# Strided attention: merged preparation, declared waits, and V loaded from the GpSimd queue

## The chip, the cores and the metric

The kernel runs on one core of a Trainium2 chip. A core has five instruction streams: TensorE (PE in the profile; its weight loads are PEld), VectorE (DVE), ScalarE (ACT), GpSimd (POOL) and SyncE (SP), and 16 DMA engines that carry data between the chip's memory and the core's SBUF. The metric is the device time in microseconds (us); lower is better. The times of the kernel before are 128.76, 128.98 and 129.75 us, with a median of 128.98.

## The reference: what is computed

Q, K and V have the shape 8 x 12 x 1024 x 64 in float32, and the stride is 64. Every query attends only to the 16 positions 0, 64, 128, ..., 960:

```
for i in range(seq):
    attend_positions = np.arange(0, seq, stride)
    q = Q[:, :, i:i + 1, :]
    k = K[:, :, attend_positions, :]
    v = V[:, :, attend_positions, :]
    scores = einsum('bhqd,bhkd->bhqk', q, k) * scale          # scale = 1/8
    weights = exp(scores - max(scores)); weights /= sum(weights) + 1e-10
    result[:, :, i, :] = einsum('bhqk,bhkd->bhqd', weights, v)
```

All of Q (25.2 MB) is read and all of the result (25.2 MB) is written. Of K and V only one row in 64 is read, 0.39 MB each, in rows of 64 floats (256 bytes) that lie 16 KB apart.

## The kernel before, in words

The 96 pairs of batch and head are worked on in 24 groups (`g`) of four heads. A group loads 1 MB of Q into one of ten buffers `qn` (`load`, L95), and stores 1 MB of the result from one of eight buffers `out_sb` (`store`, L243). Both are DMAs that SyncE issues, all on one queue and in the order in which the program names them: K, Q0, V, Q1 to Q9, and then in the loop store 0, Q10, store 1, Q11 and so on, and at the end only stores. Each of these DMAs also waits until the one eight places before it has landed.

The order of work on each engine is written out by hand (`manual_schedule`); the framework adds the waits between engines from what is read and written. Per group:

- `cast` (L188): Q is turned to bf16 in two halves, one on POOL (L191), one on ACT (L192), into one of two buffers `qb`.
- `transpose` (L194): DVE transposes it in 32 x 32 blocks into `qt` (L196).
- `scores` (L198): four matmuls against the zero-padded keys `k_t` (L203), then two exponentials on ACT (L214) into one of three weight buffers in `w_all`.
- `values` (L180): POOL multiplies a mask with the group's values into one of three buffers in `v_all` (L182). Four more columns of `v_all` give the sums of the weights.
- `outputs` (L221): eight matmuls (L228) in three parts (`c`). DVE takes the reciprocals of the sums (L236) and multiplies the first two parts (L238); for the third part ACT copies it out of PSUM (L240) and POOL multiplies it in place (L241).

The function `ahead` runs the transpose, the values and the scores of later groups before the outputs of the current one, and `cast` three groups ahead.

Ahead of the loop stand the preparations. POOL builds an identity matrix (L120, L121), copies of its columns `perm_v` (L128), and clears two thirds of `k_t` (L134). DVE clears the rest (L132) and `w_all` (L133), and builds the mask from an iota in four small operations (L136 to L139). `key_rows` (L147) casts four of K's twelve slices on ACT and transposes them on DVE; `keys` (L156) places them in `k_t` with four small copies for each half. The first four slices are done ahead of the loop, with half of the copies on DVE; the others in two lots within groups 1 to 3 and 5 to 7. V is cast on DVE (L258), and `value_rows` (L168) spreads six of its slices at a time with two matmuls (L171), each with a copy out of PSUM on DVE (L175): ahead of the loop and again in group 4.

`addr_align(128, max_nops=0)` (L87 for DVE and POOL, L102 for SyncE) makes an engine's stream go on at an aligned place in the instruction memory, by a jump.

Of the kernel before, what the change touches and what calls it, by code (L numbers as in the profile page):

```python
# [9 lines left out]

FP32 = mybir.dt.float32
BF16 = mybir.dt.bfloat16
I16 = mybir.dt.int16
I32 = mybir.dt.int32
AF = mybir.ActivationFunctionType
ALU = mybir.AluOpType
# [8 lines left out]
def _copy(nc, out: bass.AP, in_: bass.AP):  # L25

    sides = [
        mybir.BassSymbolicTensorAccessPattern(
            ap=side.ap, dtype=side.dtype, bass_ap=side,
            is_dma=True, for_custom_bir_dma=True,  # L30
        )
        for side in (in_, out)
    ]
    return nc.sync.add_instruction(
        mybir.InstDMACopy(
            name=nc.get_next_instruction_name(), engine=mybir.EngineType.SP,
            ins=sides[:1], outs=sides[1:], queue="qSPDynamicHW",
            mode="Copy",
        )
    )  # L40
# [9 lines left out]
def kernel(  # L50
# [8 lines left out]
    nc = tc.nc  # L59

    B, H, S, D = Q.shape
    NK = S // stride
# [3 lines left out]
    HG = 4  # L66
# [6 lines left out]
    OBUFS = 8  # L73

    const = ctx.enter_context(tc.tile_pool(name="const", bufs=1))
    qn_pool = ctx.enter_context(tc.tile_pool(name="qn", bufs=QBUFS))
    out_pool = ctx.enter_context(tc.tile_pool(name="outsb", bufs=OBUFS))
    qb_pool = ctx.enter_context(tc.tile_pool(name="qb", bufs=2))
# [12 lines left out]
    v_raw = const.tile([P, NC, D], FP32, name="v_raw")  # L91
    kv_src = [[stride * D, P], [2 * HG * SD, NC], [1, D]]
    qn = {}

    def load(g):  # L95
        qn[g] = qn_pool.tile([P, 32 * D], FP32, name="qn", tag="qn")
        n = P if g < 2 else 32
        _copy(nc, qn[g], _ap_with(Q, [[HG * SD // n, n], [1, HG * SD // n]], g * HG * SD))
# [10 lines left out]
    ahead4 = const.tile([P, 4], I16, name="ahead4")  # L109
    slot4 = const.tile([P, 4], I16, name="slot4")  # L110
# [15 lines left out]
    for c in range(2):  # L126
        for a in range(2):
# [5 lines left out]
    nc.vector.memset(w_all, 0.0)  # L133
    nc.gpsimd.memset(k_t[:, 8:NG], 0.0)  # L134

    nc.vector.tensor_single_scalar(out=slot4, in_=ahead4, scalar=48, op=ALU.bitwise_and)  # L136
# [7 lines left out]
    v_rep = const.tile([P, NC, 2, D], BF16, name="v_rep")  # L144


    def key_rows(m):  # L147
        part = slice(4 * m, 4 * m + 4)
# [7 lines left out]
    def keys(m, c):  # L156
        for s in range(4):
            src, dst, col = 32 * (2 * c + s % 2), 32 * (2 * (s % 2) + s // 2), NK + 32 * s
            op = nc.vector.tensor_copy if m == 0 and s >= 2 else nc.scalar.copy
            op(  # L160
                k_t[dst : dst + 32, 8 * m + c : 8 * m + 8 : 2, :, col : col + NK],
                k_r[src : src + 32, 4 * m : 4 * m + 4].rearrange(
                    "p n (a k f) -> p a n f k", a=2, f=2
                )[:, s // 2],
            )


    def value_rows(n):  # L168
        for c in range(2):
            vp = psum_sc.tile([P, NC // 2, D], FP32, name="vp", tag="sc")  # L170
            nc.tensor.matmul(  # L171
                vp, lhsT=perm_v[:, c].rearrange("p a b e k -> p (a b e k)"),
                rhs=v_bf[:, 6 * n : 6 * n + 6], start=True, stop=True,
            )
            nc.vector.tensor_copy(out=v_rep[:, 6 * n : 6 * n + 6, c], in_=vp)  # L175

    qb, qt, wt, vb, rec, out_sb = {}, {}, {}, {}, {}, {}


    def values(g):  # L180
        vb[g] = v_bufs[g % 3]
        nc.gpsimd.tensor_tensor(  # L182
            out=vb[g][:, 0 : 4 * D].rearrange("p (s d) -> p s d", s=4), in0=mask,
            in1=v_rep[:, g // 2, g % 2].unsqueeze(1).to_broadcast([P, 4, D]),
            op=ALU.mult,
        )

    def cast(g):  # L188
        qb[g] = qb_pool.tile([P, 32 * D], BF16, name="qb", tag="qb")
        half = 16 * D  # L190
        nc.gpsimd.tensor_copy(out=qb[g][:, 0:half], in_=qn[g][:, 0:half])  # L191
        nc.scalar.copy(qb[g][:, half:], qn[g][:, half:])  # L192

    def transpose(g):  # L194
        qt[g] = qt_pool.tile([P, 32 * D], BF16, name="qt", tag="qt")
        nc.vector.transpose(qt[g].bitcast(I32), qb[g].bitcast(I32))  # L196

    def scores(g):  # L198
        sc = psum_sc.tile([P, 512], FP32, name="sc", tag="sc")
        q = qt[g]  # L200
        for e in range(2):
            for f in range(2):
                nc.tensor.matmul(  # L203
                    sc, lhsT=k_t[:, g, f, NK * (1 - e) : NK * (1 - e) + P],
                    rhs=_ap_with(
                        q, [q.ap[0], [D, 8], [16 * D, 2], [2, 32]],
                        extra_offset=8 * D * e + f,
                    ),
                    start=e + f == 0, stop=e + f == 2,
                )  # L210
        w = wt[g] = w_bufs[g % 3]
        for a in range(2):
            wa = w[64 * a : 64 * a + 64]
            nc.scalar.activation(  # L214
                out=_ap_with(wa, [wa.ap[0], [P, 8], [1, 2], [2, 32]], extra_offset=64 * a),
                in_=sc[64 * a : 64 * a + 64].rearrange("p (t x q) -> p t x q", t=8, x=2),
                func=AF.Exp, bias=0.0, scale=scale,
            )


    def outputs(g, c):  # L221
        if c == 0:
            out_sb[g] = out_pool.tile([P, 4, 8, D], FP32, name="out_sb", tag="out_sb")
# [12 lines left out]
        nc.vector.reciprocal(r, ps[:, 0:n, 4 * D : 4 * D + 4])  # L236
        if c < 2:
            nc.vector.tensor_tensor(out=to, in0=o, in1=by, op=ALU.mult)  # L238
        else:
            nc.scalar.copy(to, o)  # L240
            nc.gpsimd.tensor_tensor(out=to, in0=to, in1=by, op=ALU.mult)  # L241

    def store(g):  # L243
        o = out_sb[g]
        _copy(
            nc,
            _ap_with(out, [[16 * D, P], [2 * SD, 2], [1, 16 * D]], g * HG * SD),
            _ap_with(o, [o.ap[0], [1, 1], [1, 32 * D]]),
        )

    key_rows(0)
    keys(0, 0)
    cast(0)
    transpose(0)
    keys(0, 1)
# [19 lines left out]
    for g in range(NG):  # L275
        if g > 0:
            ahead(g)
        for c in range(3):
            outputs(g, c)
        if g == 0:  # L280
            ahead(g)
        if g in (1, 5):
            key_rows(g // 4 + 1)
        if g in (2, 3, 6, 7):
            keys(g // 4 + 1, g % 4 - 2)
        if g == 4:
            value_rows(1)
        store(g)
        if g + QBUFS < NG:
            load(g + QBUFS)  # L290
# [33 lines left out]
```

## Time and profile before

| | |
|---|---|
| median of 3 runs | 128.98 us (128.76 to 129.75) |
| the profiled execution's own time | 128.94 us |
| its span, first to last instruction | 127.2 us |
| mean granted TensorE clock | 0.835 |
| busy: PE, DVE, ACT, POOL | 51%, 69%, 68%, 62% of the span |
| moved by DMA | 51.20 MB, of it 25.95 MB read from memory and 25.17 MB written |
| issue to landing, median: Q load, store, K, V | 14.7, 13.5, 4.5, 7.4 us |

The span is one profiled execution; the 1.74 us between it and that execution's time lie ahead of the first instruction or behind the last. "Busy" counts instructions that do work; DMA issues and waits are not in it. A line of the table by stage gives a stretch in us, its length, the busy time of PE, PEld, DVE, ACT and POOL with the count of instructions, the clock granted to TensorE, the mean busy share of the 16 DMA engines (it can be a little over 1, as packets overlap) and the GB/s that they moved. A line in order of time gives start, duration, engine, line, operation, output and input, and in brackets the idle time before it and what ended it. "SPq" is SyncE issuing DMAs; the transfer itself comes later.

### The profile page before, as it was taken

How to read it: one execution, taken by the hardware profiler on the slowest of the kernel's cores; microseconds unless marked ns; L12 is line 12 of the kernel's file. 1: busy time of each engine (PE TensorE's matmuls, PEld its weight loads, DVE VectorE, ACT ScalarE, POOL GpSimd, SP SyncE). 2: the span in 40 equal slices, each digit the busy share in tenths (PEclk: the TensorE clock that was granted, in tenths of full speed). 3: DMA queues.
4: the chain of work that ended last, by engine and by line, in shares of the span. 5: the costliest groups of instructions: out<-in, count | busy, mean ns of one | idle time of the engine just before them, and what ended most of it. 6: DMA issues, size and time to landing. Idle time of an engine off the chain costs nothing.

```text
span 127.2 us, 1226 instructions
## 1 busy us (share of the span) xinstructions
PE 64.3 (51%) x292; PEld 30.2 (24%) x292; DVE 88.4 (69%) x162; ACT 86.0 (68%) x120; POOL 79.5 (62%) x84
## 2 busy tenths in 40 slices
PE   0006548196757619662787636666463797430000
PEld 0002223042323304330333313233232343110000
DVE  4956592769698786877887889797988876760000
ACT  4151917957999986999958997979798765620000
POOL 6941818645855994595867896969889673454000
PEclk9999999755699995999657999999999558975555
DMA  2999999989998998998999989989999999999980
GB/s 67 374 329 474 464 412 423 464 381 394 451 451 381 459 464 343 487 433 376 500 387 405 497 353 438 461 374 451 428 402 451 397 433 420 425 433 417 428 350 26
DMA packets 7911, 51.20 MB, mean 403 GB/s; under 512 B 3872, under 2 KB 3872, under 8 KB 3872
## 3 DMA queue, kind: packets, MB, share of 16 engines
q1 hardware_dynamic: 7904, 51.12, 96.5%
q8 instruction: 2, 0.03, 0.1%
q14 instruction: 5, 0.04, 0.1%
HBM read 25.95 MB, written 25.17 MB: 402 GB/s over the span
## 4 chain that ended last, share of the span: by engine, by line
POOL 35%; issue 32%; DMA 15%; DVE 4%; PE 2%; ACT 1%; POOLq 1%; SPq 0%; DVEq 0%
POOL qb L191 14%; POOL out_sb L241 12%; POOL v_all L182 9%; DMA out_dram<-out_sb 9%; DMA qn<-in_Q_dram 5%; PE sc L203 1%; POOLq L319 1%; DVE out_sb L238 1%; DVE qt L196 1%; DVE v_rep L175 1%; ACT qb L192 1%; PE vp L171 1%; ACT out_sb L240 1%; DVE rec L236 0%; SPq L100 0%
## 5 line engine op out<-in xcount | busy, mean ns | idle before, releaser
L228 PE MATMUL o_ps<-v_all,w_all 128*128 128x260 bf16 x192 | 38.4, 320 | 37.1 <-DVE out_sb L238 32.8
L241 POOL TENSOR_TENSOR out_sb<-out_sb,rec 128x768 f32<-128x768 f32 x24 | 35.3, 1471 | 29.8 <-ACT out_sb L240 29.8
L238 DVE TENSOR_TENSOR out_sb<-o_ps,rec 128x768 f32<-128x768 f32 (+1 forms) x48 | 39.6, 825 | 1.7
L214 ACT ACTIVATE w_all<-sc 64x512 bf16<-64x512 f32 x48 | 35.2, 734 | 5.5 <-PE sc L203 4.9
L203 PE MATMUL sc<-qt,k_t 128*128 128x512 bf16 x96 | 32.0, 466 | 10.7 <-DVE qt L196 10.7
L196 DVE STREAM_TRANSPOSE qt<-qb 128x1024 int32<-128x1024 int32 x24 | 29.6, 1232 | 10.8 <-ACT qb L192 5.7
L228 PEld LDWEIGHTS <-w_all 128*128 128x128 bf16 x192 | 18.9, 109 | 60.3 <-DVE out_sb L238 41.2
L240 ACT COPY out_sb<-o_ps 128x768 f32<-128x768 f32 x24 | 19.2, 798 | 16.1 <-DVE rec L236 15.8
L191 POOL CAST qb<-qn 128x1024 bf16<-128x1024 f32 x24 | 24.9, 1036 | 4.7 <-DMA qn<-in_Q_dram 4.7
L192 ACT CAST qb<-qn 128x1024 bf16<-128x1024 f32 x24 | 25.0, 1045 | 0.7
L236 DVE RECIPROCAL rec<-o_ps 128x12 f32<-128x12 f32 (+1 forms) x72 | 15.1, 210 | 6.3 <-PE o_ps L228 5.8
L182 POOL TENSOR_TENSOR v_all<-mask,v_rep 128x256 bf16<-128x256 bf16 x24 | 16.0, 668 | 0.6 <-DVE v_rep L175 0.6
L203 PEld LDWEIGHTS <-k_t 128*128 128x128 bf16 x96 | 10.8, 113 | 21.6 <-ACT k_t L160 8.1
L160 ACT COPY k_t<-k_r 32x128 bf16<-32x128 bf16 x20 | 5.9, 295 | 2.1 <-DVE k_r L150 1.9
L134 POOL MEMSET k_t<- 128x4608 bf16 x1 | 3.9, 3938 | 0.0
L175 DVE CAST v_rep<-vp 128x384 bf16<-128x384 f32 x4 | 2.2, 542 | 1.9 <-PE vp L171 1.8
L149 ACT CAST k_bf<-k_raw 128x256 bf16<-128x256 f32 x3 | 1.2, 406 | 3.2 <-DMA k_raw<-in_K_dram 3.2
L150 DVE STREAM_TRANSPOSE k_r<-k_bf 128x128 int32<-128x128 int32 x3 | 0.9, 310 | 2.3 <-ACT k_bf L149 2.3
L136 DVE TENSOR_SCALAR slot<-ahead 128x4 int16<-128x4 int16 x1 | 2.5, 2482 | 0.0
L171 PE MATMUL vp<-v_bf,perm_v 128*128 128x384 bf16 x4 | 1.6, 412 | 1.1 <-DVE v_rep L175 0.6
L132 DVE MEMSET k_t<- 128x1152 uint32 x1 | 1.0, 1018 | 1.6 <-PEq L305 1.6
L149 ACT ACT_TABLE_LOAD x1 | 1.3, 1283 | 0.7 <-PEq L305 0.7
(15 smaller groups left out, 5.7 us busy)
## 6 DMA issues: line engine op xcount, KB each, us to landing
qn<-in_Q_dram SPq DMA_DIRECT2D x24, 1024.0 KB, 14.7
out_dram<-out_sb SPq DMA_DIRECT2D x24, 1024.0 KB, 13.5
k_raw<-in_K_dram SPq DMA_DIRECT2D x1, 384.0 KB, 4.5
v_raw<-in_V_dram SPq DMA_DIRECT2D x1, 384.0 KB, 7.4
```

Source lines behind the costliest of these rows:

```text
L160: op(k_t[dst : dst + 32, 8 * m + c : 8 * m + 8 : 2, :, col : col + NK], k_r[src : src + 32, 4 * m : 4 * m + 4].rearrange("p n (a k f) -> p ...
L182: nc.gpsimd.tensor_tensor(out=vb[g][:, 0 : 4 * D].rearrange("p (s d) -> p s d", s=4), in0=mask, in1=v_rep[:, g // 2, g % 2].unsqueeze(1).t ...
L191: nc.gpsimd.tensor_copy(out=qb[g][:, 0:half], in_=qn[g][:, 0:half])
L192: nc.scalar.copy(qb[g][:, half:], qn[g][:, half:])
L196: nc.vector.transpose(qt[g].bitcast(I32), qb[g].bitcast(I32))
L203: nc.tensor.matmul(sc, lhsT=k_t[:, g, f, NK * (1 - e) : NK * (1 - e) + P], rhs=_ap_with(q, [q.ap[0], [D, 8], [16 * D, 2], [2, 32]], extra_ ...
L214: nc.scalar.activation(out=_ap_with(wa, [wa.ap[0], [P, 8], [1, 2], [2, 32]], extra_offset=64 * a), in_=sc[64 * a : 64 * a + 64].rearrange( ...
L228: nc.tensor.matmul(ps[:, i, 0 : 4 * D + 4], lhsT=wt[g][:, i0 + i], rhs=vb[g], start=True, stop=True,)
L236: nc.vector.reciprocal(r, ps[:, 0:n, 4 * D : 4 * D + 4])
L238: nc.vector.tensor_tensor(out=to, in0=o, in1=by, op=ALU.mult)
L240: nc.scalar.copy(to, o)
L241: nc.gpsimd.tensor_tensor(out=to, in0=to, in1=by, op=ALU.mult)
```

## The change

V's load moves from SyncE's queue to POOL's, and its position there is ahead of POOL's other preparation. The aligning jumps are taken out on all three engines.

The preparation is merged. All of `k_t` is cleared by one memset on DVE. The mask comes from one reduction over the identity on DVE and two copies on POOL, in place of an iota and four operations on DVE. The remaining eight slices of K are cast and transposed in one lot in group 1, and their copies, eight in place of sixteen, go two to a group in groups 2 to 5. The first key copies that were on DVE are on POOL, and V's cast too; on POOL it stands behind the cast of Q1. The two matmuls of `value_rows` write two banks of one PSUM tile of the output pool, and one copy on DVE takes both.

Buffers that came from rotating pools (`qn`, `qb`, `out_sb`) are fixed tiles, and dependencies that follow from others are declared as none (`implied`): a reloaded Q buffer on its old load and casts, a cast on the casts two groups before, exponentials and values on those of three groups before, and ACT's copy and POOL's product on the store that used the buffer last. In exchange the transpose of group `g`, for `g` of 10 and more, waits for store `g - 10`, which frees the buffer that DVE fills next.

```diff
-    for engine in (nc.vector, nc.gpsimd):
-        engine.addr_align(128, max_nops=0)
...
+    def implied(ins, earlier, why):
+        tc.declare_no_dep(ins.ins, earlier.ins, reason=why)
...
     nc.sync.dma_start(k_raw, _ap_with(K, kv_src))
     load(0)
-    nc.sync.addr_align(128, max_nops=0)
-    nc.sync.dma_start(v_raw, _ap_with(V, kv_src))
+    nc.gpsimd.dma_start(v_raw, _ap_with(V, kv_src))
...
-    nc.gpsimd.iota(ahead4, pattern=[[-16, 4]], base=64, channel_multiplier=1)
...
-    nc.vector.memset(k_t[:, 0:8], 0.0)
+    nc.vector.memset(k_t, 0.0)
     nc.vector.memset(w_all, 0.0)
-    nc.gpsimd.memset(k_t[:, 8:NG], 0.0)
-
-    nc.vector.tensor_single_scalar(out=slot4, in_=ahead4, scalar=48, op=ALU.bitwise_and)
-    nc.vector.tensor_single_scalar(out=s_sel, in_=slot4, scalar=0, op=ALU.is_equal)
-    nc.vector.tensor_copy(out=v_all[:, :, 4 * D :], in_=s_sel.unsqueeze(1).to_broadcast([P, 3, 4]))
-    nc.vector.tensor_copy(out=mask, in_=s_sel.unsqueeze(2).to_broadcast([P, 4, D]))
+
+    nc.vector.tensor_reduce(
+        out=s_sel, in_=identity.rearrange("p (h s k) -> p s h k", h=2, s=4),
+        op=ALU.max, axis=mybir.AxisListType.XY,
+    )
+    nc.gpsimd.tensor_copy(out=v_all[:, :, 4 * D :], in_=s_sel.unsqueeze(1).to_broadcast([P, 3, 4]))
+    nc.gpsimd.tensor_copy(out=mask, in_=s_sel.unsqueeze(2).to_broadcast([P, 4, D]))
...
-            op = nc.vector.tensor_copy if m == 0 and s >= 2 else nc.scalar.copy
+        op = nc.gpsimd.tensor_copy if part is first and s >= 2 else nc.scalar.copy
...
     def value_rows(n):
+        vp = psum_o.tile([P, 3, 512], FP32, name="o_ps", tag="o")
+        rows = vp[:, 0:2, 0 : NC // 2 * D].rearrange("p c (n d) -> p c n d", d=D)
         for c in range(2):
-            vp = psum_sc.tile([P, NC // 2, D], FP32, name="vp", tag="sc")
...
-            nc.vector.tensor_copy(out=v_rep[:, 6 * n : 6 * n + 6, c], in_=vp)
+        nc.vector.tensor_copy(
+            out=v_rep[:, 6 * n : 6 * n + 6].rearrange("p n c d -> p c n d"), in_=rows
+        )
...
+        if g - 2 >= OBUFS:
+            tc.add_manual_dep(
+                turned.ins, stored[g - 2 - OBUFS].ins.name,
+                mybir.DependencyInfo(mybir.DependencyClass.Sync, mybir.DependencyReason.ANTI),
+                reason="frees the output buffer that VectorE fills next",
+            )
...
     cast(1)
-    nc.vector.tensor_copy(out=v_bf, in_=v_raw)
+    nc.gpsimd.tensor_copy(out=v_bf, in_=v_raw)
     value_rows(0)
...
-        if g in (1, 5):
-            key_rows(g // 4 + 1)
-        if g in (2, 3, 6, 7):
-            keys(g // 4 + 1, g % 4 - 2)
+        if g == 1:
+            key_rows(rest)
+        if 2 <= g < 6:
+            for i in range(2 * g - 4, 2 * g - 2):
+                keys(rest, i // 4, i % 4)
```

More of the change, by code (lines that the diff above doesn't have):

```diff
@@ L12 @@
 BF16 = mybir.dt.bfloat16
-I16 = mybir.dt.int16
 I32 = mybir.dt.int32
@@ L84 @@
     ctx.enter_context(tc.manual_schedule())
-    for engine in (nc.vector, nc.gpsimd):
-        engine.addr_align(128, max_nops=0)
     k_raw = const.tile([P, NC, D], FP32, name="k_raw")
     v_raw = const.tile([P, NC, D], FP32, name="v_raw")
+    qn_bufs = [const.tile([P, 32 * D], FP32, name=f"qn{i}") for i in range(QBUFS)]
+    qb_bufs = [const.tile([P, 32 * D], BF16, name=f"qb{i}") for i in range(2)]
+    out_bufs = [const.tile([P, 4, 8, D], FP32, name=f"out_sb{i}") for i in range(OBUFS)]
     kv_src = [[stride * D, P], [2 * HG * SD, NC], [1, D]]
-    qn = {}
+    qn, stored, cast_by, scaled = {}, {}, {}, {}
+    loaded, raised, masked = {}, {}, {}
+    def implied(ins, earlier, why):
+        tc.declare_no_dep(ins.ins, earlier.ins, reason=why)
     def load(g):
-        qn[g] = qn_pool.tile([P, 32 * D], FP32, name="qn", tag="qn")
+        qn[g] = qn_bufs[g % QBUFS]
         n = P if g < 2 else 32
-        _copy(nc, qn[g], _ap_with(Q, [[HG * SD // n, n], [1, HG * SD // n]], g * HG * SD))
+        loaded[g] = _copy(nc, qn[g], _ap_with(Q, [[HG * SD // n, n], [1, HG * SD // n]], g * HG * SD))
+        if g >= QBUFS:
+            for earlier in (loaded[g - QBUFS], *cast_by[g - QBUFS]):
+                implied(loaded[g], earlier, "the store before it has waited for both casts")
     nc.sync.dma_start(k_raw, _ap_with(K, kv_src))
     load(0)
-    nc.sync.addr_align(128, max_nops=0)
-    nc.sync.dma_start(v_raw, _ap_with(V, kv_src))
+    nc.gpsimd.dma_start(v_raw, _ap_with(V, kv_src))
     for g in range(1, QBUFS):
@@ L144, with key_rows @@
     v_rep = const.tile([P, NC, 2, D], BF16, name="v_rep")
-    def key_rows(m):
-        part = slice(4 * m, 4 * m + 4)
+    def key_rows(part):
         nc.scalar.copy(k_bf[:, part], k_raw[:, part])
@@ L186, in values @@
         )
+        if g >= 3:
+            implied(masked[g], masked[g - 3], "the matmuls between them")
     def cast(g):
-        qb[g] = qb_pool.tile([P, 32 * D], BF16, name="qb", tag="qb")
+        qb[g] = qb_bufs[g % 2]
         half = 16 * D
-        nc.gpsimd.tensor_copy(out=qb[g][:, 0:half], in_=qn[g][:, 0:half])
-        nc.scalar.copy(qb[g][:, half:], qn[g][:, half:])
+        cast_by[g] = (
+            nc.gpsimd.tensor_copy(out=qb[g][:, 0:half], in_=qn[g][:, 0:half]),
+            nc.scalar.copy(qb[g][:, half:], qn[g][:, half:]),
+        )
+        if g >= 2:
+            for h in range(2):
+                for e in range(2):
+                    implied(cast_by[g][h], cast_by[g - 2][e], "the transpose between them")
     def transpose(g):
         qt[g] = qt_pool.tile([P, 32 * D], BF16, name="qt", tag="qt")
-        nc.vector.transpose(qt[g].bitcast(I32), qb[g].bitcast(I32))
+        turned = nc.vector.transpose(qt[g].bitcast(I32), qb[g].bitcast(I32))
+        if g - 2 >= OBUFS:
[3 more added lines that the diff above has]
+                reason="frees the output buffer that VectorE fills next",
+            )
     def scores(g):
@@ L211, in scores @@
         w = wt[g] = w_bufs[g % 3]
+        raised[g] = []
         for a in range(2):
             wa = w[64 * a : 64 * a + 64]
-            nc.scalar.activation(
+            raised[g].append(nc.scalar.activation(
                 out=_ap_with(wa, [wa.ap[0], [P, 8], [1, 2], [2, 32]], extra_offset=64 * a),
@@ L217, in scores @@
                 func=AF.Exp, bias=0.0, scale=scale,
-            )
+            ))
+            for earlier in raised.get(g - 3, ()):
+                implied(raised[g][a], earlier, "the matmuls between them")
     def outputs(g, c):
         if c == 0:
-            out_sb[g] = out_pool.tile([P, 4, 8, D], FP32, name="out_sb", tag="out_sb")
+            out_sb[g] = out_bufs[g % OBUFS]
             rec[g] = rec_pool.tile([P, 8, 4], FP32, name="rec", tag="rec")
@@ L239, in outputs @@
         else:
-            nc.scalar.copy(to, o)
-            nc.gpsimd.tensor_tensor(out=to, in0=to, in1=by, op=ALU.mult)
+            copied = nc.scalar.copy(to, o)
+            scaled[g] = nc.gpsimd.tensor_tensor(out=to, in0=to, in1=by, op=ALU.mult)
+            for past in range(g - OBUFS, -1, -OBUFS):
+                for earlier in (stored[past], scaled[past]):
+                    implied(copied, earlier, "VectorE has waited for the store")
+                implied(scaled[g], stored[past], "VectorE has waited for the store")
     def store(g):
         o = out_sb[g]
-        _copy(
+        stored[g] = _copy(
             nc,
@@ L249, in store @@
         )
-    key_rows(0)
-    keys(0, 0)
+    first, rest = slice(0, 4), slice(4, NC)
+    key_rows(first)
+    for s in range(4):
+        keys(first, 0, s)
     cast(0)
     transpose(0)
-    keys(0, 1)
+    for s in range(4):
+        keys(first, 1, s)
     scores(0)
     cast(1)
-    nc.vector.tensor_copy(out=v_bf, in_=v_raw)
+    nc.gpsimd.tensor_copy(out=v_bf, in_=v_raw)
     value_rows(0)
```

25 lines of the change are left out of this document (9 added, 16 removed).

## The prediction

> **What bounds the kernel now.** I read the page's summary of the span and of the queues first, because it says whether any compute engine can be the limit.
>
> ```profile
> span 127.2 us, 1226 instructions
> DMA  2999999989998998998999989989999999999980
> GB/s 67 374 329 474 464 412 423 464 381 394 451 451 381 459 464 343 487 433 376 500 387 405 497 353 438 461 374 451 428 402 451 397 433 420 425 433 417 428 350 26
> q1 hardware_dynamic: 7904, 51.12, 96.5%
> ```
>
> No compute engine is above 69% busy, but the 16 DMA engines are full from the second of the 40 slices to the last but two, and the one queue q1 fills 96.5% of them. The table by stage says how evenly:
>
> ```profile
> 20.00:30.00 10.00, 5.58 (x22) 2.35 (x20) 5.79 (x10) 8.25 (x11) 7.05 (x8) 0.69 0.99 424
> 60.00:70.00 10.00, 7.60 (x32) 3.67 (x33) 8.22 (x17) 7.89 (x10) 7.88 (x9) 0.66 1.01 428
> 110.00:115.00 5.00, 1.71 (x9) 0.65 (x8) 2.73 (x7) 1.60 (x2) 2.15 (x2) 0.75 1.01 426
> 115.00:120.00 5.00, 0.00 (x0) 0.00 (x0) 0.00 (x0) 0.00 (x0) 0.79 (x1) 0.50 1.03 431
> ```
>
> The last two columns are the DMA share and GB/s: 424 to 431 whether the engines compute or not. So the time is: start of the flow, plus 51.12 MB at about 426 GB/s, plus what is lost to slow stretches, plus the end. The chain that ended last names POOL for 35%, but it follows the last instruction back through waits that a full DMA queue hides; I don't price by it.
>
> The only slow stretches are at the start, where K and then V are moved in rows of 256 bytes:
>
> ```profile
> 1.50:2.00 0.50, 0.00 (x0) 0.00 (x0) 0.39 (x1) 0.50 (x1) 0.36 (x3) 1.00 0.16 38
> 2.00:2.50 0.50, 0.00 (x0) 0.00 (x0) 0.50 (x1) 0.01 (x1) 0.50 (x4) 1.00 0.26 65
> 2.50:3.00 0.50, 0.00 (x0) 0.00 (x0) 0.23 (x2) 0.00 (x0) 0.50 (x3) 1.00 0.98 233
> 3.00:3.50 0.50, 0.00 (x0) 0.00 (x0) 0.50 (x1) 0.00 (x0) 0.50 (x1) 1.00 1.11 245
> ...
> 6.50:7.00 0.50, 0.00 (x0) 0.00 (x0) 0.43 (x4) 0.00 (x0) 0.11 (x1) 1.00 1.06 274
> 7.00:7.50 0.50, 0.00 (x0) 0.00 (x0) 0.47 (x4) 0.01 (x1) 0.00 (x0) 1.00 1.04 237
> ```
>
> From 1.5 to 4.5 us the half-microseconds carry 38, 65, 233, 245, 329 and 361 GB/s, 0.64 MB instead of 1.28: 1.5 us lost, 0.7 of it in the first two, where the engines are nearly idle. From 6 to 9 us the rates 352, 274, 237, 341, 360 and 399 lose 0.7 us. These 2.2 us are all that an earlier or better start can win back. At the end the flow thins out from 122.5 us on and the span ends 127.2; nothing edited lies there.
>
> **How much lateness is hidden.** The SyncE queue in order of time:
>
> ```profile
> 2.91 9.84 SPq L34 DMA_DIRECT2D qn<-in_Q_dram  x9
> 21.14 0.63 SPq L34 DMA_DIRECT2D out_dram<-out_sb  x1
> 21.87 0.55 SPq L34 DMA_DIRECT2D qn<-in_Q_dram  x1
> 28.77 0.59 SPq L34 DMA_DIRECT2D out_dram<-out_sb  x1
> 33.65 0.59 SPq L34 DMA_DIRECT2D out_dram<-out_sb  x1
> ```
>
> (Loads between the last two are left out.) When the first store is issued at 21.14, 11.27 MB have been asked for (K, V, ten loads of 1.05 MB) and 7.55 MB moved (mean rates of the stages up to there), so 3.72 MB are queued, to 29.9 us at 425 GB/s. That store and the load after it carry the queue to 34.8. The second store comes at 28.77, 6.0 us before; the third at 33.65 against 39.8, the fourth at 38.15 against 44.7. So 6.0 us is the thinnest cover. A new request brings its first bytes about 1.1 us after issue (K: issued 0.73, first packet in the trace 1.83), so 4.9 us of lateness at the start is free; beyond that each microsecond costs one. At the end the last store is issued at 115.8 with flow until 125: some 7 us of cover.
>
> **The change, part by part.**
>
> *Loads of Q on SyncE.* V (0.39 us) and the jump before it (idle from 1.94 to 2.47) leave the queue; loads 1 to 9 are issued up to 1 us earlier. From 2.5 us on the DMA engines are full, so this is worth 0. K keeps its issue at 0.73, so the flow starts at 1.83 as before: 0.
>
> *V's transfer.* Its 0.39 MB stay. On a queue of its own the rows could fill gaps: at best its 0.7 us come back, and K's gap as well (below, as a rival); at worst its rows move at the slowest rate of K's start that has many rows under way, 65 GB/s, 6.0 us in place of 1.6 at 245: 4.4 us lost. The nearest row is the same transfer on SyncE, so I take most of the old cost and a part of the overlap: −0.4 us.
>
> *Writing V's request on POOL.* No row shows POOL issuing a DMA. Low: SyncE's 0.39 us for the same V. [...]
>
> *V's cast behind POOL's second Q cast.* Before, VectorE cast V at 11.13 and the first `v_all` stood at 13.53 + 0.67 = 14.2. Now: Q1 lands and POOL casts it from 12.31 to 13.35; V's cast, 768 × 1.01 ns, 0.78, to 14.1; two matmuls of 0.41, to 15.0; the merged copy out of PSUM, at most 2 × 0.56, to 16.1; `v_all` 0.67, to 16.8. The first store is 2.6 us later. The 4.9 us hide it: 0, with 2.3 us left over. Without that cover it would cost 2.6.
>
> *Preparation on VectorE.* Memsets start at 0.73 (as ScalarE, which has no jump, does now) instead of 1.61; k_t costs 3 × 1.02, w_all 1.34, to 5.1; a small reduction 0.3. Gone are four small operations, one of which stood still:
>
> ```profile
> 2.67 3.94 POOL L134 MEMSET k_t<- 128x4608 bf16 x1
> 2.90 1.34 DVE L133 MEMSET w_all<- 128x1536 uint32 x1 [0.27 <-issue]
> 4.15 2.48 DVE L136 TENSOR_SCALAR slot<-ahead 128x4 int16<-128x4 int16 x1
> ```
>
> A four-element operation of 2.48 us that ends (6.63) as POOL's memset ends (6.61) was held by it. K's transpose can start near 5.7 instead of 7.15, but Q0 lands at 8.2: 0. [...]
>
> *Merged keys, dropped waits.* Sixteen key copies of 0.295 us become eight, two key casts and transposes become one: at most 3 us off ScalarE between 27 and 60 us, beside full DMA: 0. The dropped waits (load on casts, cast on cast, copy on store) were satisfied when reached: 0. One wait moves ahead: the transpose of group g now waits for store g − 10, before it and the reciprocal and product queued behind it on VectorE. Closest: the transpose at 103.07 needs the store issued at 79.39; with the longest landing of any store, 19.6, it is there at 99.0, 4.1 us early. 0.
>
> Sum: 128.94 (span 127.2 and 1.74 around it, in the profiled execution; the median is 128.98) − 0.4 = **128.5**.
>
> **Rivals.**
>
> *V fills K's idle start (faster).* If POOL's rows are ready near 2 us, they move while K's request is only trickling. For: shares of 0.16 and 0.26 from 1.5 to 2.5. Then V's whole cost, 0.92 us of bytes and 0.7 lost, goes: 128.9 − 1.6 = 127.3. Against: POOL must write 1,536 rows in about 1 us. 0.15.
>
> *V lands late (slower).* Two queues share each DMA engine, which has 96 of V's rows. Handed out in runs, V is through quickly; handed out one row for each packet of the other queue, whose packets here are 8 KB (0.31 us each, 16 per engine in Q0 and Q1) and then 32 KB (1.22 us), the rows that K's small ones don't match wait 5 us for the first 16 and 1.2 us each after that. The point is V's landing at 13.35 + 2.3 = 15.6 us: each microsecond later costs one. Four rows among the 32 KB packets put it near 20: 133.3; thirty are worth 36 us. For: nothing in the trace shows two data queues at once, and the request starts late. Against: before, V lands at 9.9. 0.12. [...]
>
> *Rows from the second queue are dearer.* The 4.4 us end above, or half the old rate, 1.6 us: 130.5 to 133.3. 0.07.
>
> *The declarations or merges change nothing that is late.* Same time as the forecast but without the overlap: 128.9, within the forecast's case.
>
> **How the numbers follow.** Forecast 0.64, its own range 127.9 to 129.5 (V's overlap from 0.7 to a loss of half a microsecond); the rivals 0.15, 0.12 and 0.07; 0.02 for something else. One per cent, 1.3 us, is about what a measurement here can tell from no change (the three runs span 128.76 to 129.75). Faster 0.15, same 0.65, slower 0.20. The range 127.3 to 131.0 leaves out the late V, the dearest rows and a little below.
>
> **What would show it.** Right: DMA near 426 GB/s from 10 to 122 us, no slice under 9 tenths around 25 to 40, V landed by 13 us, the first store near 23 to 24. Wrong: DMA thinning out between 27 and 40 us with a late first store (V or POOL's request), or rates above 100 GB/s before 2.5 us (V fills the gap). V's cast waiting on its DMA beyond 15.6 us would undo the forecast.

## The result, and the profile after

The changed kernel takes **129.55 us** (median of 22 executions, 129.13 to 130.03), the kernel before 128.96 us on the same chip (22 executions, 128.46 to 129.79). The ratio is **1.0037, with a 95% interval of 1.0022 to 1.0051**: 0.6 us slower, where 0.4 us faster was forecast. The change is small but clear of the noise (0.28 to 0.66 us by the interval). One execution among all runs, the profiled one of the changed kernel with V back on SyncE's queue, was disturbed (157.92 us) and is left out of its comparison.

The profiled execution took 129.48 us. Its span is 127.35 us, so 2.13 us lie outside the span, where the kernel before had 1.77 (128.94 less 127.17). The page of the changed kernel, summary of the span and queues:

```profile
span 127.3 us, 1114 instructions
DMA  2999999997998989989989989999999899999991
GB/s 53 365 338 479 422 401 443 381 494 324 499 412 368 517 360 401 463 373 435 476 368 448 455 381 471 440 383 466 432 383 476 373 419 425 430 419 427 430 394 51
q1 hardware_dynamic: 6352, 50.73, 95.6%
q0 software_dynamic: 112, 0.39, 0.9%
```

The DMA engines bound the kernel as before. The one seven among the slices, at 28.6 to 31.8 us with 324 GB/s, follows a slice with 494: one row of 16 packets of 32 KB more or less is 165 GB/s of a slice, so this is where packets fall, not a gap. (The prediction named "no slice under 9 tenths around 25 to 40" as a sign of being right; with this seven and the eights it isn't met, but slices of eight stand there in the kernel before too.) V's 0.39 MB stand in a line of their own, q0. The bytes and the form of the flow are the same, so 0.6 us must lie in a slightly lower rate, at the ends, or outside the span. The table by stage of the changed kernel (after the name of the stretch and its length come PE, PEld, DVE, ACT and POOL, then the granted clock, the DMA share and GB/s):

```profile
12.00:28.00 16.00, 9.30 (x32) 3.52 (x31) 8.81 (x14) 10.09 (x13) 8.61 (x10) 0.94 0.99 418
28.00:60.00 32.00, 19.56 (x96) 9.51 (x95) 26.86 (x49) 29.02 (x40) 23.96 (x24) 0.87 1.01 426
60.00:115.00 55.00, 33.04 (x166) 15.90 (x164) 44.10 (x84) 41.63 (x53) 41.10 (x39) 0.87 1.01 425
```

The same stretches of the kernel before:

```profile
12.00:28.00 16.00, 9.64 (x34) 3.98 (x33) 9.40 (x17) 10.54 (x14) 8.76 (x10) 0.87 1.00 428
28.00:60.00 32.00, 19.29 (x91) 9.10 (x88) 26.00 (x48) 29.03 (x48) 22.16 (x22) 0.85 1.00 421
60.00:115.00 55.00, 34.04 (x167) 16.50 (x167) 44.77 (x86) 42.54 (x53) 41.31 (x41) 0.85 1.01 426
```

From 28 us on, loads and stores are mixed and the rates agree. Between 12 and 28 us only Q is loaded, and there the changed kernel moves 418 GB/s in place of 428, though its engines compute no more. One row of 16 packets is 33 GB/s of such a stretch, so this line alone proves little; it says where to look. The trace's packet records are sharper: in that stretch, a 32 KB packet takes 1,246 ns (median of 204) after and 1,218 ns (median of 209) before. In the mixed stretches both have 1,219 ns.

What the prediction had said would be seen came out as follows. The changed kernel's SyncE queue in order of time (start, duration; loads of Q left out) and POOL's first work:

```profile
21.94 0.62 SPq L33 DMA_DIRECT2D out_dram<-out_sb  x1
...
29.57 0.59 SPq L33 DMA_DIRECT2D out_dram<-out_sb  x1
...
34.61 0.59 SPq L33 DMA_DIRECT2D out_dram<-out_sb  x1
```

```profile
1.25 1.18 POOL L105 DMA_DIRECT2D v_raw<-in_V_dram  x1 [0.81 <-POOLq L331]
...
11.84 1.03 POOL L195 CAST qb<-qn 128x1024 bf16<-128x1024 f32 x1 [1.87 <-DMA qn<-in_Q_dram]
12.82 0.82 POOL L283 CAST v_bf<-v_raw 128x768 bf16<-128x768 f32 x1
```

The first three stores are 0.80, 0.80 and 0.96 us later than before, far inside the 4.9 us of cover. POOL needs 1.18 us for V's request, and V's cast follows the cast of Q1 without a gap, so it doesn't wait for its DMA.

### The profile page after: what moved, and what is told of

It reads as the page before. It is cut to its first block, busy times and chain, and to the rows that moved or that the text cites. A ratio compares the mean times of both kernels' runs of the same rounds, so it can differ in the third digit from the quotient of the medians.

```text
span 127.3 us, 1114 instructions
## 1 busy us (share of the span) xinstructions
PE 63.3 (50%) x292; PEld 29.6 (23%) x292; DVE 85.6 (67%) x151; ACT 84.6 (66%) x111; POOL 79.2 (62%) x90
## 4 chain that ended last, share of the span: by engine, by line
DMA 37%; DVE 17%; ACT 11%; PE 10%; POOL 8%; issue 3%; POOLq 1%; SPq 1%; DVEq 0%
DMA qn<-in_Q_dram 37%; DVE out_sb L256 9%; DVE qt L205 5%; PE o_ps L246 5%; PE sc L218 4%; ACT out_sb L258 4%; ACT w_all L230 3%; POOL out_sb L259 3%; DVE rec L254 3%; ACT qb L196 2%; POOL qb L195 2%; POOL v_all L183 2%; PE o_ps L170 1%; POOLq L345 1%; ACT k_t L158 1%
## 5 line engine op out<-in xcount | busy, mean ns | idle before, releaser
L246 PE MATMUL o_ps<-v_all,w_all 128*128 128x260 bf16 x192 | 37.2, 311 | 36.5 <-DVE out_sb L256 30.8
L218 PE MATMUL sc<-qt,k_t 128*128 128x512 bf16 x96 | 32.0, 466 | 10.6 <-DVE qt L205 10.6
L158 ACT COPY k_t<-k_r 32x256 bf16<-32x256 bf16 (+1 forms) x12 | 4.4, 366 | 1.1 <-DVE k_r L149 1.0
L174 DVE CAST v_rep<-o_ps 128x768 bf16<-128x768 f32 x2 | 1.9, 958 | 4.7 <-PE o_ps L170 4.7
L131 DVE MEMSET k_t<- 128x3456 uint32 x1 | 2.9, 2938 | 1.5 <-PEq L331 1.5
L148 ACT CAST k_bf<-k_raw 128x256 bf16<-128x256 f32 (+1 forms) x2 | 1.0, 512 | 3.1 <-DMA k_raw<-in_K_dram 3.1
L170 PE MATMUL o_ps<-v_bf,perm_v 128*128 128x384 bf16 x4 | 1.6, 508 | 1.6 <-POOL v_bf L283 1.2
L105 POOL DMA_DIRECT2D v_raw<-in_V_dram x1 | 1.2, 1181 | 0.8 <-POOLq L331 0.8
L149 DVE STREAM_TRANSPOSE k_r<-k_bf 128x128 int32<-128x128 int32 (+1 forms) x2 | 0.7, 370 | 1.4 <-ACT k_bf L148 1.4
```

What stands on the lines that cost most here:

```text
L158: op(k_t[dst : dst + 32, 2 * part.start + c : 2 * part.stop : 2, :, col : col + NK], k_r[src : src + 32, part].rearrange("p n (a k f) -> p ...
L218: nc.tensor.matmul(sc, lhsT=k_t[:, g, f, NK * (1 - e) : NK * (1 - e) + P], rhs=_ap_with(q, [q.ap[0], [D, 8], [16 * D, 2], [2, 32]], extra_ ...
L246: nc.tensor.matmul(ps[:, i, 0 : 4 * D + 4], lhsT=wt[g][:, i0 + i], rhs=vb[g], start=True, stop=True,)
```

## The experiments

The account that comes out of them, in us (after less before), is this; the parts below say how each term was found.

| term | where it is seen | size |
|---|---|---|
| Q's buffers at another place in SBUF | 32 KB packets of 1,246 ns for 1,218: 0.4 us of the flow | +0.7 by the times of runs with and without |
| POOL's jump gone | between the last data and the end of the span | −0.3 |
| VectorE's stream shorter | 0.36 more outside the span | 0 to +0.36, open |
| V on POOL's queue | no gain in the flow | 0 to +0.3 by the times |
| declared waits, merged preparation | nothing found | 0 |

The first two terms add up to 0.4, and 0.28 to 0.66 was measured. So the two terms that start from 0 can't both stand at their upper ends, though each figure here has an error of some tenths.

### V's queue alone, in both directions

The changed kernel with V on SyncE's queue again:

```diff
-    nc.gpsimd.dma_start(v_raw, _ap_with(V, kv_src))
+    nc.sync.dma_start(v_raw, _ap_with(V, kv_src))
```

> The changed kernel with V's load back on SyncE's queue, between Q0 and Q1; no jumps, merged preparation and declared waits stay. Theory Q (V's own queue costs the 0.6 us): back to 128.8 to 129.0, and the packets of 32 KB take 1.218 us between 12 and 28 us, as in the kernel before. Theory R (the rest of the change costs it): 129.5, and 1.24 us per packet.

Measured: 129.33 us (median of 11 executions), ratio to the kernel before 1.0034 (1.0011 to 1.0056). The loss stays, so most of it isn't V's queue. The 32 KB packets between 12 and 28 us still take 1,246 ns.

The kernel before, with V on POOL's queue and nothing else changed:

```diff
-    nc.sync.dma_start(v_raw, _ap_with(V, kv_src))
+    nc.gpsimd.dma_start(v_raw, _ap_with(V, kv_src))
```

> The kernel before with one edit: V is loaded on the GpSimd queue; jumps and preparation stay. Theory Q: 129.5, and packets of 1.24 us between 12 and 28 us. Theory R: 128.95, and 1.218 us.

Measured: 129.75 us, ratio 1.0047 (1.0018 to 1.0075). The twelve executions fall into two groups, five between 128.75 and 129.16 and seven between 129.70 and 130.17. The profiled one is of the first group (129.05 us, packets of 1,219 ns). Its beginning in order of time:

```profile
3.51 1.19 POOL L103 DMA_DIRECT2D v_raw<-in_V_dram  x1 [3.07 <-issue]
...
6.30 3.93 POOL L134 MEMSET k_t<- 128x4608 bf16 x1
...
6.46 4.83 DVE L160 COPY k_t<-k_r 32x128 bf16<-32x128 bf16 x2
```

POOL stands still until 3.51 behind its jump, then writes the request, and its memset of `k_t` moves to 6.30. Two key copies of VectorE, which take 0.22 us each in the kernel before, begin at 6.46 and end at 11.29. By the trace's records the first takes 3.85 us and ends at 10.31, as the memset ends (10.23); the second takes 0.97 us beside POOL's cast of Q0 (10.18 to 11.21). The two on ScalarE, which begin at 6.46 as well, take 0.60 us together. So in the old preparation the queue change pushes POOL's memset onto VectorE's copies; the merged preparation, which has no such memset on POOL, takes that collision away. Why seven of the twelve executions are 0.8 us longer wasn't seen in a profile and stays open.

### The jumps

The kernel before without its three aligning jumps:

```diff
-    for engine in (nc.vector, nc.gpsimd):
-        engine.addr_align(128, max_nops=0)
...
-    nc.sync.addr_align(128, max_nops=0)
```

> The kernel before without the three aligning jumps, nothing else. Theory Q: 128.9 to 129.0, within 0.1% of the kernel before, since the first load is issued ahead of SyncE's jump in both. Theory R, if it is the missing jumps: 129.5.

Measured: 128.41 us, ratio 0.9962 (0.9938 to 0.9986): this part of the change does win, 0.2 to 0.8 us by the interval. In the profiled executions it is 0.44 us, nearly all of it at the end: the last data land at 125.44 us (before 125.47), but from there to the end of the span it is 1.28 us where the kernel before takes 1.69. To tell the three jumps apart, only POOL's was taken out:

```diff
-    for engine in (nc.vector, nc.gpsimd):
+    for engine in (nc.vector,):
```

> The kernel before without POOL's aligning jump; those of VectorE and SyncE stay. With all jumps POOL's last entries stand still for 0.4 us and the span ends 1.69 us behind the last data; without any, 1.28. If POOL's own jump is the cause: about 1.28. If it is another one: 1.69.

Measured in one execution: 128.85 us (129.07 before), and 1.29 us from the last data to the end. The last instructions of all engines stand under the line that closes the kernel. The view by source line gives operation, count, shortest, median and longest in ns, then start of the first and of the last in us. POOL's in the kernel before:

```profile
L319 POOLq EVENT_SEMAPHORE  x4: 17/17/17, 126.1 to 127.1; - x4
L319 POOLq DRAIN  x3: 40/78/1577, 114.3 to 126.5; - x3
```

and in the kernel without POOL's jump:

```profile
L319 POOLq EVENT_SEMAPHORE  x4: 17/17/17, 126.4 to 127.0; - x4
L319 POOLq DRAIN  x3: 40/78/1577, 114.0 to 126.8; - x3
```

From the last drain to the last semaphore it is 0.6 us in the one and 0.2 in the other. In the trace's records, POOL's last drain ends at 126.57 in the kernel before and its next instruction begins at 126.97; without the jump these are 126.85 and 126.90. So with the jump at POOL's beginning goes a standstill of 0.4 us at its end, and the other engines wait for it: in the kernel before their last semaphores stand at 127.1 us, as POOL's does. All four profiles with POOL's jump take 1.67 to 1.86 us from the last data to the end, all others 1.24 to 1.40. Why it stands still so late is not shown. The changed kernel takes 1.38 us from the last data to the end. It gains 0.3, not 0.4; of the missing 0.1, half is one instruction of POOL that clears semaphores and takes 142 ns in place of 96 with V on its queue. This kind of end is seen in all runs with V there and without the jump (1.36 to 1.40).

### Where V's request stands on POOL

The next theory was that the request on POOL at 1.25 us, beside SyncE's first, slowed the start of K's rows (172 GB/s from 2.5 to 3.0 us, before 233). Here POOL writes it after the copies of `perm_v`, at 2.07:

```diff
-    nc.gpsimd.dma_start(v_raw, _ap_with(V, kv_src))
     for g in range(1, QBUFS):
         load(g)
...
                 in_=id_v[:, c, :, a].unsqueeze(2).to_broadcast([P, 2, 2, NK]),
             )
+    nc.gpsimd.dma_start(v_raw, _ap_with(V, kv_src))
```

> The changed kernel with V's load still on the GpSimd queue, but behind POOL's identity and its copies, some 1.5 us later. If writing V's request beside K's is what slows K's start (17, 54 and 172 GB/s from 1.5 to 3 us against 38, 65 and 233), the rates go back to those of the kernel before and 0.2 us come back: 129.3. If V's request has nothing to do with K's start: rates as in the changed kernel, 129.5. If V's own queue costs by where its rows fall among Q0 and Q1, the loss at 9 to 10 us grows.

Measured: 129.42 us, ratio 1.0037 (1.0017 to 1.0057). From 1.5 to 5 us it moves 234 GB/s, nearly the 241 of the kernel before, where the changed kernel moves 218 (0.2 us of flow less), but the time is the same within 0.13. This rate also varies with V on SyncE (212 to 253 GB/s in seven profiles) at least as much as with V on POOL in the changed kernel's forms (218 to 236 in five). The theory fell.

A theory made on the way fell too: that packets are slower where the 16 engines run closer together in time. Their starts within one packet's time spread over 0.98 us in the kernel before (1,218 ns) and 0.55 after (1,246 ns), but over 0.76 in this run, at 1,246 ns, and over 0.69 in the kernel before with V on POOL, at 1,219 ns. The two runs below say it more sharply: 0.42 us at 1,219 ns with the buffers moved, 0.96 at 1,246 ns in the kernel before with 128 bytes.

### Where the buffers lie

What differs in a 32 KB packet of Q is where it goes. From a rotating pool, the first `qn` stood at byte 53,248 of each partition, 13 times 4,096, and the others in steps of 8,192 from it. As fixed tiles, declared right behind `v_raw`, they start at byte 22,656, which is 128 more than a multiple of 256. (These addresses were settled when the kernels were compiled, and no view shows them. The sizes of the tiles ahead, each counted up to a multiple of 32 bytes, which is an assumption of this count, give the same distance between the two, 36,736 less 6,144 = 30,592 bytes, which is 119.5 times 256.) One unused tile ahead of them moves them in the changed kernel to 24,576, 6 times 4,096:

```diff
     v_raw = const.tile([P, NC, D], FP32, name="v_raw")
+    const.tile([P, 960], BF16, name="pad")
     qn_bufs = [const.tile([P, 32 * D], FP32, name=f"qn{i}") for i in range(QBUFS)]
```

> The changed kernel with an unused tile of 1,920 bytes per partition ahead of the Q buffers, so that these and the output buffers begin at multiples of 4,096 bytes of a partition, as they do in the kernel before; in the changed kernel they begin 2,176 bytes behind such a multiple. Theory A (the place of the buffers makes the Q packets slow): the packets of 32 KB between 12 and 28 us take 1.218 us instead of 1.24, 16 of them on each engine save 0.4 us: 129.1. Theory S (the 16 engines run closer together in time): the packets stay at 1.24, 129.5.

In the kernel before, an unused tile of 128 bytes puts them to 53,376, off by 128 as in the changed kernel:

```diff
+    const.tile([P, 64], BF16, name="pad")
     qn = {}
```

> The kernel before with an unused tile of 128 bytes per partition ahead of the Q buffers, which moves them and the output buffers 128 bytes behind a multiple of 4,096; nothing else. Theory A: packets of 1.24 us between 12 and 28 us, 129.4. Theory S: 1.218 us and 129.0.

And one of 256 bytes puts them to 53,504, a multiple of 256 but not of more:

```diff
+    const.tile([P, 128], BF16, name="pad")
     qn = {}
```

> The kernel before with an unused tile of 256 bytes per partition ahead of the Q buffers, so that these begin 256 bytes behind a multiple of 4,096. If what counts is a multiple of 256: packets of 1.218 us between 12 and 28 us, as before. If it is a coarser multiple (512 to 4,096): about 1.24.

Measured:

| kernel | first buffer, less a multiple of 256 | us | ratio to before | 32 KB packet, 12 to 28 us |
|---|---|---|---|---|
| before | 0 | 128.96 | | 1,218 ns |
| after | 128 | 129.55 | 1.0037 (1.0022 to 1.0051) | 1,246 ns |
| after, moved | 0 | 128.87 | 0.9983 (0.9969 to 0.9997) | 1,219 ns |
| before, 128 bytes | 128 | 129.82 | 1.0057 (1.0039 to 1.0076) | 1,246 ns |
| before, 256 bytes | 0 | 128.91 (one execution) | | 1,218 ns |

The view of DMA from 12 to 28 us shows the same without packet records. Its lines give the packets, MB, and the time that the packets took as a share of 16 engines' 16 us. The kernel before:

```profile
q1 hardware_dynamic: 317, 6.85, 99.9%
```

The changed kernel:

```profile
q1 hardware_dynamic: 300, 6.69, 99.5%
```

The changed kernel with its buffers moved:

```profile
q1 hardware_dynamic: 320, 7.01, 102.2%
```

The kernel before with 128 bytes ahead of its buffers:

```profile
q1 hardware_dynamic: 298, 6.59, 98.0%
```

The kernel before with 256 bytes:

```profile
q1 hardware_dynamic: 321, 7.05, 102.7%
```

Engine time for 32,768 bytes is share × 256 us ÷ MB × 0.032768 MB. That gives 1,223, 1,248, 1,223, 1,247 and 1,222 ns in this order: two values, and the one beside the multiple of 256 is 2.0% above the other. The packets themselves say 2.3%.

So the place of the buffers costs 0.68 us in the changed kernel and 0.86 in the kernel before, by the medians. Of it 16 packets for each engine (Q2 to Q9) × 28 ns = 0.45 us are placed in the stretch of loads alone. The bytes that had moved agree: from 12 to 40 us the changed kernel, its forms with V later and with all waits made, and the kernel before with 128 bytes fall 0.38 to 0.41 us of flow behind the kernel before, and the others whose V has landed by 12 us between −0.01 and 0.08. So does the end of the flow, though it scatters: those four have their last data at 125.68 to 126.57 us (median 125.88), the nine at a multiple of 256 at 124.92 to 125.79 (median 125.44). The rest, 0.3 to 0.5, isn't placed. The buffers of the result, and every other tile declared behind the unused one, are moved by the same bytes, so they weren't tried apart from Q's. But the packets of the stretch in which there are only stores take 311 ns for 8 KB in all five kernels, and in the mixed stretch the 32 KB packets take 1,219 ns in all five.

So it is shown that the place costs time, and that the 32 KB packets are longer by it where only loads are under way; why they are is not shown.

### What lies outside the span

With its buffers moved, the changed kernel has a span 0.45 us shorter than the kernel before (medians of 126.75 and 127.2), but its time is only 0.09 shorter. All forms of the changed kernel so far had 2.13 to 2.17 us outside the span, all forms of the kernel before 1.77 to 1.81. The first suspect was the length of the streams, through the declared waits. The changed kernel with none of them declared:

```diff
     def implied(ins, earlier, why):
-        tc.declare_no_dep(ins.ins, earlier.ins, reason=why)
+        pass
```

> The changed kernel in which nothing is declared as implied, so that the framework adds those waits again. Between the span and the execution's own time lie 2.13 us in the changed kernel and 1.78 in the kernel before, with and without jumps. If the shorter streams (ScalarE 119 entries against 165) are behind these 0.35 us, they go back to 1.78 and the time to 129.2; if the waits mattered inside the span, the time grows; by the forecast's reasoning neither: 129.5.

Measured: 129.69 us, ratio 1.0059 (1.0038 to 1.0081), six executions, with 2.15 us outside the span. The recorded entries of the streams grow from 89 to 99 (SyncE), 109 to 146 (POOL) and 119 to 156 (ACT); VectorE's stay at 184. Neither the waits nor these three lengths matter to the time outside; and with all waits made again the time is 0.14 us more, which is no measurable difference.

V's queue doesn't matter to it either. The changed kernel with its buffers moved and V on SyncE:

```diff
+    const.tile([P, 960], BF16, name="pad")
...
-    nc.gpsimd.dma_start(v_raw, _ap_with(V, kv_src))
+    nc.sync.dma_start(v_raw, _ap_with(V, kv_src))
```

> The changed kernel with the aligning tile and with V back on SyncE's queue: merged preparation, declared waits and no jumps remain. If the place of the buffers (0.4 us) and V's queue (0.1 to 0.3) are what made the change slower, this is 128.4, like the kernel before without its jumps, or lower if the merged preparation is worth anything. If the merged preparation and declared waits cost time themselves, 128.9 or more.

Measured: 128.83 us, ratio 0.9980 (0.9955 to 1.0005), with 2.17 us outside. Beside the run with V on POOL (128.87) this is the same, and it lies between the two forecasts.

What was left is VectorE, whose stream the merged preparation shortens from 209 entries to 184. The last kernel with 24 memsets of one element more, which do no useful work:

```diff
     nc.vector.memset(w_all, 0.0)
+    spare = const.tile([P, 24], FP32, name="spare")
+    for i in range(24):
+        nc.vector.memset(spare[:, i : i + 1], 0.0)
```

> The changed kernel with aligned buffers and V on SyncE's queue, and with 24 memsets of one element each on VectorE behind its two large ones, into a tile that nothing reads. They do no useful work; they make VectorE's stream about as long as in the kernel before (209 entries against 184). Theory L (the 0.36 us between span and execution time come with the length of VectorE's stream, the only count that stayed short when the declared waits were added again): 1.78 us outside the span and 128.45. Otherwise: 2.15 us outside, and 128.8, as the memsets lie ahead of the landing of Q0.

Measured: **128.54 us, ratio 0.9966** (0.9945 to 0.9987), with 1.78 us outside. The time outside the span falls from 2.17 to that of the kernel before, so it follows VectorE's stream: its length, or where it ends. Why was not shown. The median of the time is 0.29 us lower, but that work added for nothing makes the kernel faster isn't shown: the intervals of the two ratios overlap (0.9955 to 1.0005 without the memsets), and the next run doesn't repeat it.

No instruction lies outside the span, but the trace has DMA packets there, of a kind that it calls `instruction`. One of 8 KB behind the end of the span (127.65 to 128.20 us in the kernel before) stands in all four kernels with POOL's jump and in no other. So it goes with the jump, and not with the 0.36: this run has 1.78 without it.

The same with V on POOL's queue, that is, the whole change with the buffers moved and the 24 memsets:

> The changed kernel whole, V on the GpSimd queue, with aligned buffers and the 24 one-element memsets on VectorE. If the place of the buffers (0.68 us between the changed kernel and its aligned form) and the length of VectorE's stream (0.36) are all that made the change slower, and V's queue is worth nothing either way: 128.5, as with V on SyncE's queue. If V's queue costs: 128.7 or more; if it helps: 128.3 or less.

Measured: 128.87 us, ratio 0.9993 (0.9978 to 1.0008), with 1.77 us outside and 1.37 from the last data to the end. The time outside the span falls here too, but the time doesn't: without the memsets it was 128.87 as well (ratio 0.9983), and the median of the span grows from 126.75 to 127.1. So 0.36 us less outside the span came with 0.29 us less time in one pair and with none in the other. For a cost speaks that the changed kernel with its buffers moved and V on SyncE (128.83) isn't as fast as the kernel before without its jumps (128.41), though the intervals of these two ratios overlap as well. So whether the 0.36 is paid stays open. The kernel with V on SyncE is 0.3 us faster by both the medians and the ratios, whose intervals just overlap. With the pair above (0.04) and that of the first run (0.2), V on POOL's queue costs between 0 and 0.3 us and wins nothing; 0.08 of it is the slower end (1.37 for 1.29 us).

The two fastest versions are the kernel before without its jumps (128.41 us, ratio 0.9962) and the changed kernel with V on SyncE, buffers moved and 24 idle memsets (128.54, ratio 0.9966). They differ by all of the declared waits and all of the merged preparation, and not in time.

## Why the prediction was right or wrong, point by point

- **What bounds the kernel: right.** Only DMA does. No delay of an engine in the first 40 us was paid for.
- **The flow, "51.12 MB at about 426 GB/s", and loads of Q on SyncE, "0": the step that failed first.** The prediction priced when the loads are issued, and that is 0. But it has no part for the fixed tiles, which put Q's buffers at another place, and the flow was taken to go on at its old rate. It didn't: a 32 KB packet takes 2.3% more between 12 and 28 us, 0.4 us of flow and about 0.7 us of time. That the buffers move by 128 bytes against a multiple of 256 was to be had before any run, from the sizes of the tiles; what this costs was not, since no row of the kernel before shows it. There was no term for it in the sum and no rival.
- **The end, "nothing edited lies there": failed.** With the jump at POOL's beginning goes a standstill of 0.4 us in its last instructions, so taking it out wins about 0.3. And "1.74 around it" was carried over as a constant, but outside the span it went from 1.77 to 2.13 us with the shorter stream on VectorE; whether this costs time stays open.
- **V's transfer, "−0.4 us": wrong.** The old rows' cost wasn't won back. V's first data packet begins at 6.19 us, and until 9.68 its packets lie beside those of Q. From 6 to 10 us the half-microseconds of the changed kernel carry 1.37 MB, those of the kernel before 1.40: the slow stretch stays. Taking the most of the old cost as paid left 0.4 to win, and 0 to +0.3 was measured.
- **V's request on POOL: hidden, as the sum has it.** No row of the kernel before shows POOL writing a request, and any size above the low bound was the author's estimate. It took 1.18 us, three times that bound of 0.39. It started at 1.25, and POOL's work ahead of Q0 was done at 7.5, before the casts of Q0 began (8.15 on ACT, 8.25 on POOL).
- **V's cast: mechanism right, size wrong.** The estimate was a first store 2.6 us later; it was 0.80 later. Q1 landed sooner (its cast began at 11.84, not 12.31), the cast behind it took 0.82 us, and the merged copy out of PSUM 0.96, where 1.12 was allowed. The cover hid it, as said.
- **Preparation on VectorE: right at 0.** `k_t`'s memset took 2.94 us (3.06 estimated), though it started at 1.53 rather than 0.73. K's transpose was at 6.13 (forecast 5.7) and Q0 was still later.
- **Merged keys, dropped and added waits, "0": right.** Without the declarations the time is the same, and among the waits of VectorE in the changed kernel none is for a DMA, so the wait for store `g − 10` cost nothing.
- **The rivals.** V didn't fill K's idle start: from 1.5 to 2.5 us the changed kernel moves 17 and 54 GB/s, less than before. V wasn't late: the page has 9.4 us from issue to landing, so 10.6. Dearer rows: not seen as a cost of the size priced there (1.6 to 4.4). One of the prediction's readings is off: of K's 1.5 us lost, its own rows give 0.9 to the first two half-microseconds (0.05 MB instead of 0.43), not 0.7; the sum doesn't use it.

The two halves of the start, in the changed kernel's table by stage, with the point at which the flow is up:

```profile
1.50:2.00 0.50, 0.00 (x0) 0.00 (x0) 0.47 (x1) 0.50 (x1) 0.50 (x1) 1.00 0.07 17
2.00:2.50 0.50, 0.00 (x0) 0.00 (x0) 0.50 (x1) 0.02 (x1) 0.50 (x2) 1.00 0.21 54
2.50:3.00 0.50, 0.00 (x0) 0.00 (x0) 0.50 (x1) 0.00 (x0) 0.42 (x2) 1.00 0.74 172
3.00:3.50 0.50, 0.00 (x0) 0.00 (x0) 0.50 (x1) 0.00 (x0) 0.44 (x4) 1.00 1.14 260
```

and the landing of K and V, in us behind the KB:

```profile
k_raw<-in_K_dram SPq DMA_DIRECT2D x1, 384.0 KB, 4.3
v_raw<-in_V_dram POOLq DMA_DIRECT2D x1, 384.0 KB, 9.4
```

V's rows went as 96 packets of 4,096 bytes, 16 rows each; over 16 engines that is six for each on average. They weren't handed out one row for each packet of the other queue, as the rival had it at its worst: between 6.19 and 9.68 us they lie among Q's packets of 8 KB, and V landed at 10.6.

The sum of the prediction was 128.94 − 0.4. The profiled pair alone splits into 128.94 + 0.49 (last data later) − 0.31 (shorter end) + 0.36 (outside the span) = 129.48, but single executions scatter by as much as each of these (those of the kernel before from 128.46 to 129.79). With the terms from many executions it is 128.94 + 0.7 − 0.3 = 129.3, and the median is 129.55; the 0.2 between them leaves room for a part of V's 0 to 0.3 and of the 0 to 0.36, and not for both in full. In this kernel, which its DMA bounds, nearly every step that was worked out carefully was worth 0, and what moved the time was in places that had been passed over in half a sentence or not at all.

## What to carry to other kernels

Where DMA bounds a kernel, look first at what an edit does to the transfers themselves: here, turning pooled buffers into fixed tiles moved them by 128 bytes against a multiple of 256, and that cost more (0.68 us by the medians of the runs with and without) than the edits of instructions won (0.3, by POOL's jump). Check the addresses of large DMA buffers after every edit of the tiles ahead of them. And price the two ends, with what lies outside the span, as terms of their own: when everything between is hidden, an alignment jump at the start of a stream is among what is left to see (here 0.4 us at the end). Where a stretch outside the span moves, ask whether the time moves with it before counting it.

## What the runs showed of the hardware that was not expected

- Loads of 32 KB packets into rows of 8 KB take 1,246 ns where the rows begin 128 bytes beside a multiple of 256, and 1,218 where they don't, with only loads under way; beside stores, 1,219 in either case. Stores of such rows show no difference (311 ns for 8 KB). Rows at an odd multiple of 256 bytes were as fast as at multiples of 4,096 (1,218 ns, one execution).
- A jump at the start of POOL's stream is paid for at the end as well: 0.4 us between its last drain and its next instruction, and 0.05 us without the jump. An `instruction` packet of 8 KB behind the end of the span goes with it.
- The execution time is 1.77 to 1.81 us longer than the span where VectorE's stream has about 209 entries, and 2.13 to 2.17 where it has 184. The streams of SyncE, POOL and ACT changed by up to 37 entries with no such effect. Whether the time itself follows stays open.
- POOL writes a request of 1,536 rows of 256 bytes in 1.18 us; SyncE issues the same in 0.39 in the kernel before.
- Beside POOL's memset of 3.93 us, a key copy on VectorE took 3.85 us rather than 0.22, and the next, beside POOL's cast of Q0, 0.97; the memset of `w_all` on VectorE that lay beside POOL's memset in the kernel before wasn't held (1.34 us).
